# Half 1's input products of the long convolution beside its recurrence, and its gating beside its delta rule

## The chip, the cores and the metric

The kernel runs on one core of a Trainium2 chip. The metric is the device time of one execution in microseconds; of several runs of the kernel before, the median is 3470.67 us. The engines are TensorE (PE in the rows, PEld for its weight loads), VectorE (DVE), ScalarE (ACT), GpSimd (POOL) and SyncE (SP). Each engine works through its own list of instructions in order. Weights are loaded by SP, rows of the expert tables are gathered by GpSimd, and both kinds of transfer share the core's 16 DMA engines.

## The reference

512 tokens of 1024 features, in float32, go through three blocks: (1) feed-forward, a mixer, feed-forward; (2) a mixer and a product-key mixture of experts (PEER); (3) retention, a state-space scan and a feed-forward. The change concerns the two mixers of blocks 1 and 2. Cut to these:

```python
# block 1: proj = x @ w_in -> q, f, i, g, conv_val, conv_gate
f = lb + (1 - lb) * sigmoid(f_raw);  k = 1 - f;  log_f = log(f)
o = hgrn2_chunkwise(heads(q), heads(k), heads(i_val), heads(log_f))   # the recurrence
o_a = rms(o) * hgrn_norm_g * sigmoid(g_out)
u = conv_val * sigmoid(conv_gate)                                     # input of the convolution
c = depthwise_conv(u, conv_w, width=31) + conv_b                      # along the tokens
mix = concat([o_a, silu(layer_norm(c))]) @ w_out

# block 2: p = h @ w_in
uv = gelu(p[..., COL_GM:COL_Q]);  u, v = uv[..., :512], uv[..., 512:]
v = rms_norm(v, gm_norm_w)                                            # in chunks of 128, heads of 64
s = einsum('hts,bnshd->bnthd', tril(ws), v) + bs;  y_a = u * s        # the gating
qkv = silu(short_conv(p[..., COL_Q:COL_Z], conv_w))
o = gated_delta_rule(l2(q), l2(k), v, g, beta);  y_b = rms_norm(o) * silu(z)
x = x + gt1 * (concat([y_a, y_b]) @ w_out)
h2 = modulate(rms_norm(x));  ids, gates = peer_routing(h2)            # 8 heads, 16 experts each
ff = sum(gates * gelu(h2 . peer_u[ids]) * peer_v[ids])
```

## The kernel before

The tokens are handled in two halves of 256 (`self.hf` is 0 or 1), each of two tiles of 128, one half behind the other. First half 0 goes through blocks 1 and 2 up to the routing. Then `experts` runs the 512 gather steps of half 0's experts beside half 1's blocks 1 and 2, and after that half 1's experts beside half 0's block 3. This change lies in the first of these two stages for the most part: half 1's mixers run there while half 0's gather steps fill in.

A gather step (`gather_steps`, L1155) is a gather of 128 rows of 4 KB, 0.524 MB, issued by GpSimd (L1164) up to 8 steps ahead, and one use of it: a `u_step` multiplies and sums on DVE (L1171); a `v_step` adds a scaled row to the sum on DVE (L1194), or on PE as two 128x512 products with a diagonal (L1186 builds it on ScalarE, L1188 multiplies). After 16 u-steps ScalarE applies gelu (L1174).

Where the steps stand is decided when the program is built. `tick(d, load)` adds `d * z * rate` to a credit, less `load`, and lets steps in as long as the credit covers them; `z` and the share of v-steps on PE come from `ZONE` by phase (h the recurrence, d the delta rule, m the mixer of block 2). Every tile of weights ticks 3 with a load of 1.46, every PSUM tile ticks `self.beat`, which is 1.7 in the recurrence and in the delta rule and 0 elsewhere. A second means, `idle(d)`, takes pieces from a generator `self.side` when a PSUM tile is taken: `d` is `self.gap`, from `GAP`. Until now `side` served feed-forwards of the other half alone. In the end a scheduler puts the instructions of each engine into one list, and that list is what runs.

In half 1 products are whole float32 products (`self.exact`): one matmul instruction leaves two records in the trace. `g_fm` (L256) makes feature-major products, eight instructions for one weight tile, `g_tm` (L278) token-major ones, four a tile and half. A weight tile is 0.524 MB.

Around the change, the order in half 1 is as follows. `_hgrn` (L527): products f, then the input products of the convolution (L571 to L576: `pv` and `pg`, their sigmoid `csg`, the product into `uT`), then g, q, v; then the recurrence over the two tiles (from L591), in whose first steps k is transposed (L596), k and q are multiplied (L604), decays are summed by `Mseg` (L614) and products of decayed operands follow (L631); `head_norm` closes each tile. The convolution over `uT` follows. `_mixer2` (L790): products of q, k, v, gates of the delta rule, z; then `_gating` (L839): product v (L855), product u (L856), for each tile a normalisation (L859), the product with `ws` (L863), the bias (L865), the product with u (L867), then transposes (`put_mix`, L835); then `_delta` (L888). Its head loads the constants `PM`, `tri` and `later` (L170), sums g (L900), transposes q, k, v (L915, L935), and inverts a triangular matrix by doubling, level after level (L986, L992, L995), each a chain of three products with DVE and ScalarE between them.

In half 0 the same functions run with products in parts (L280 to L282), with no gather steps beside them.

Of the kernel before, what the change touches and what calls it, by code (L numbers as in the profile page):

```python
# [21 lines left out]
NT = 4          # token tiles  # L22
NH = 2          # token tiles of a half: the halves run one behind the other
# [11 lines left out]
# Costs of steps, in the unit of tick and idle: a transfer of 512 KB, a step of the routing, the end of a token tile  # L35
DMA, ROUTE, FINISH = 1.46, 0.8, 6.0
AHEAD = 8           # gathers under way ahead of their use
GB = 15             # their buffers
# the hidden blocks of the feed-forwards that run piece by piece in the gaps of the other half
ASIDE1 = (4, 4, 4, 4, 4, 2)  # L40
ASIDE3 = (4,) * 4
FIRST3 = 16          # hidden blocks of the third feed-forward of half 0 beside the last experts
ADA = 28             # tiles of the modulation beside the first feed-forward, the others beside the second
CONV_PE = (0, 2)     # blocks of the long convolution on TensorE, by half
# by phase: pace of the steps of the experts, share of their sums that TensorE takes
ZONE = dict(x=(1, 0.5), g=(1, 0.35), h=(1.15, 0.41), c=(0.43, 0.4), f=(1.43, 0), m=(1.73, 0.06), d=(1.09, 0.4),
            R=(1.09, 0.39), r=(1.33, 0.3), F3=(1.1, 0), s=(1, 0.65))
# pieces let in by gap of TensorE
GAP = dict(_0=4, l=3, h=0.74, c=0.22, m=5.53, d=0.9, r=0.5, s=1.6, _4=5.2, ln=8, l4=8)
NORM = 4.82          # pace of a normalisation  # L50
WEIGHTS = 3          # of a tile of weights in float32
# rates of the steps: modulation beside the two feed-forwards, experts during the routing
RATE_ADA, RATE_ROUTE = (0.85, 0.6), (0.92, 2.17)
# the course of the phases beside the experts, the transfers of their own, and the share of the experts' steps to fit in
# [3 lines left out]
class Ker:  # L58
    def __init__(self, ctx, tc, I):
# [3 lines left out]
        self.exact = False      # products in float32 itself, not in parts  # L63
# [14 lines left out]
        self.aux = nc.gpsimd        # for what VectorE need not do, unless GpSimd has transfers to start  # L78
        self.lull = self.gap = 0.0
        self.busy = False  # L80
        self.hook = None
        # states: of the first and of the second block, then both of the third block's retention
# [13 lines left out]
    def xt(self, es, side=None):  # L96
        """transposed activations, split in two, for one phase"""
        xp = es.enter_context(self.tc.tile_pool(name="xt", bufs=1, side=side))
        self.XH, self.XL = self.pair(xp, "X", KD)

    def pair(self, pool, name, n, **k):
        """an operand of products, n blocks: in two parts, or whole"""
# [22 lines left out]
    def course(self, i):  # L125
        """the rate that spreads the steps of the experts over a phase"""
        whole, loads, share = COURSE[i]
        self.rate, self.credit = (share * sum(f[0] for f in self.fill) + loads) / whole, 0.0

    def tick(self, d, load=0.0):  # L130
        """a phase goes on by d, with load for a transfer of its own: the steps of the other half's experts
        go in between so that the transfers are even"""
# [12 lines left out]
    def idle(self, d):  # L145
        """TensorE has little to do for d: pieces of the feed-forward set aside go in between"""
        if self.side is not None:
            self.lull += d
            while self.lull > 0.0 and self.side is not None:
                self.lull -= self.next_piece()  # L150

    def next_piece(self):
        d = next(self.side, None)
        if d is None:
            self.side = None
        return d or 0.0

# [18 lines left out]
    def rsqrt(self, out, in_, scale, eps):  # L176
        """out = (in_ * scale + eps) ** -0.5: Newton's iteration from the halved exponent"""
# [43 lines left out]
    def ahead(self):  # L221
        """of the weights of a feed-forward set aside, split the next tile and load on"""
# [9 lines left out]
    def whole(gen):  # L232
        """all pieces of a generator at once; its value"""
# [12 lines left out]
    def g_fm(self, srcs):  # L246
        """feature-major blocks: out[f, i, t] = sum_k w_i[k, f] X[t, k]; srcs [128, 8*128]"""
# [1706 lines left out]
```

## Time and profile before

| | us |
|---|---|
| median of the runs | 3470.67 |
| lowest and highest | 3467.29, 3487.89 |
| span of the profiled execution | 3464.7 |
| PE busy in it | 3023.7 (87%) |
| DVE busy | 2667.9 (77%) |
| GpSimd busy | 1439.0 (42%) |
| ScalarE busy | 1145.3 (33%) |

The span is that of one profiled execution, from its first to its last instruction. A row of the timeline gives start, duration, engine, line, operation, `out<-in`, shape and the count of equal instructions joined; in brackets the idle time before it and what ended that. A row of the windows gives the length, the busy time of each engine with its instructions, the granted PE clock (1.00 is 2.4 GHz), the share of the DMA engines in use and what they moved. The stage of half 1's first two blocks lies between about 1000 and 1930 us.

### The profile page before, as it was taken

The numbers are of one execution on the slowest core, as the hardware profiler recorded it, in microseconds if no ns is written. First come the engines' busy times: TensorE is split into PE (matmuls) and PEld (weight loads), VectorE is DVE, ScalarE is ACT, GpSimd is POOL, SyncE is SP. The second block draws the span as 40 slices with busy tenths as digits, with TensorE's granted clock in tenths as the row PEclk, the third lists the DMA queues.
The fourth block names the chain that finished last, engine by engine and source line by source line (L and its number), as shares of the span: only waits on it lengthen the run. The fifth ranks groups of instructions, "written<-read, shape, count | busy, mean of one in ns | idle before, by whom it ended". The sixth has DMA issues, their size and how long they took to land. (4 is left out here: it accounts for less than half of the span.)

```text
span 3464.7 us, 44842 instructions
## 1 busy us (share of the span) xinstructions
PE 3023.7 (87%) x15402; PEld 2350.9 (68%) x15402; DVE 2667.9 (77%) x6456; ACT 1145.3 (33%) x1687; POOL 1439.0 (42%) x1187
## 2 busy tenths in 40 slices
PE   9999999998979789987777867879797975999998
PEld 9987889888866357836354643536474745888897
DVE  7779686665588999878898999897877786566555
ACT  4454544553312242103222121112222213455554
POOL 0020000023245656655677567586767671211200
PEclk9999999999999899998899988899998987999999
DMA  8863477542389979998999899999999995644365
GB/s 312 279 194 118 131 267 233 168 161 86 105 303 357 355 263 384 409 402 325 381 326 375 335 339 391 347 368 357 333 365 359 396 409 193 182 133 139 119 188 162
DMA packets 276757, 957.10 MB, mean 276 GB/s; under 512 B 38304, under 2 KB 42144, under 8 KB 276528
## 3 DMA queue, kind: packets, MB, share of 16 engines
q0 software_dynamic: 147456, 536.94, 41.0%
q1 hardware_dynamic: 129072, 417.29, 35.6%
q8 instruction: 122, 2.00, 0.2%
q14 instruction: 107, 0.88, 0.1%
HBM read 947.81 MB, written 2.10 MB: 274 GB/s over the span
## 5 line engine op out<-in xcount | busy, mean ns | idle before, releaser
L1164 POOL DMA_INDIRECT gu<-in_peer_v,idx x512 | 633.6, 1238 | 317.1 <-issue 111.9
L1164 POOL DMA_INDIRECT gu<-in_peer_u,idx x512 | 609.3, 1190 | 349.6 <-issue 110.9
L1171 DVE SCALAR_TENSOR_TENSOR gu<-gu 128x1024 f32<-128x1024 f32 x512 | 620.7, 1218 | 59.4 <-DMA gu<-in_peer_u,idx 55.7
L203 DVE TENSOR_TENSOR wL<-wr,wH 128x1024 fp32r<-128x1024 f32 x332 | 409.1, 1234 | 249.2 <-ACT wH L202 231.9
L256 PE MATMUL ps<-XH,wr 128*128 128x256 f32 x2368 | 528.7, 383 | 0.2 <-issue 0.2
L256 PEld LDWEIGHTS ps<-XH,wr 128*128 128x128 f32 x2368 | 450.9, 192 | 73.2 <-issue 12.8
L202 ACT CAST wH<-wr 128x1024 fp32r<-128x1024 f32 x332 | 348.3, 1050 | 440.3 <-PE ps L281 217.4
L1194 DVE SCALAR_TENSOR_TENSOR gu<-gu,act 128x1024 f32<-128x1024 f32 x366 | 467.6, 1278 | 28.6 <-DMA gu<-in_peer_v,idx 23.4
L1188 PE MATMUL ps<-gu,dg 128*128 128x512 f32 x568 | 306.5, 664 | 101.8 <-DMA gu<-in_peer_v,idx 67.4
L1188 PEld LDWEIGHTS ps<-gu,dg 128*128 128x128 f32 x568 | 112.7, 212 | 206.9 <-issue 158.2
L278 PE MATMUL ps<-wr,XH 128*128 128x512 f32 x512 | 229.1, 601 | 0.0
L256 PE MATMUL ps<-XH,wH 128*128 128x256 f32 x1408 | 206.5, 289 | 16.3 <-ACT XH L116 10.0
L256 PE MATMUL ps<-XH,wL 128*128 128x256 f32 x1408 | 202.4, 287 | 1.5 <-DVE wL L203 1.2
L256 PE MATMUL ps<-XL,wH 128*128 128x256 f32 x1408 | 203.0, 288 | 0.2
L256 PEld LDWEIGHTS ps<-XH,wH 128*128 128x128 f32 x1408 | 186.6, 196 | 21.9 <-ACT XH L116 13.7
L256 PEld LDWEIGHTS ps<-XH,wL 128*128 128x128 f32 x1408 | 185.6, 196 | 2.9 <-DVE wL L203 2.7
L203 DVE TENSOR_TENSOR fL<-fr,fH 128x1024 fp32r<-128x1024 f32 x98 | 126.1, 1288 | 79.5 <-ACT fH L202 50.1
L256 PEld LDWEIGHTS ps<-XL,wH 128*128 128x128 f32 x1408 | 186.5, 197 | 0.6 <-DVE XL L118 0.6
L278 PEld LDWEIGHTS ps<-wr,XH 128*128 128x128 f32 x512 | 98.0, 193 | 122.7 <-issue 120.3
L202 ACT CAST fH<-fr 128x1024 fp32r<-128x1024 f32 x98 | 102.6, 1047 | 175.4 <-PE ps L256 58.7
L1186 ACT ACTIVATE dg<-ident,act 128x128 f32<-128x128 f32 x142 | 55.1, 400 | 312.3 <-PE ps L1188 246.5
L184 POOL TENSOR_TENSOR r<-rx,mhalf 128x1 f32<-128x1 f32 x18 | 11.9, 669 | 330.7 <-DVE rx L182 330.7
(618 smaller groups left out, 5462.4 us busy)
## 6 DMA issues: line engine op xcount, KB each, us to landing
wr<-in_wi_fm SPq DMA_DIRECT2D x112, 512.0 KB
wr<-in_wi_tm SPq DMA_DIRECT2D x96, 512.0 KB
wr<-in_wf SPq DMA_DIRECT2D x96, 512.0 KB
wr<-in_wo SPq DMA_DIRECT2D x64, 512.0 KB
wa<-in_wada SPq DMA_DIRECT2D x48, 512.0 KB
wr<-in_f2g SPq DMA_DIRECT2D x44, 512.0 KB
wr<-in_f2u SPq DMA_DIRECT2D x44, 512.0 KB
wr<-in_f2d SPq DMA_DIRECT2D x44, 512.0 KB
```

The costliest lines, as they stand in the source:

```text
L184: nc.gpsimd.tensor_tensor(out=out, in0=x, in1=self.mhalf[:p, :].to_broadcast(list(out.shape)), op=ALU.pow)
L202: self.nc.scalar.copy(H, raw)
L203: self.nc.vector.tensor_tensor(out=L, in0=raw, in1=H, op=ALU.subtract)
L256: nc.tensor.matmul(ps[:, i * TH:(i + 1) * TH], a[:, k * P:(k + 1) * P], b[:, k, :], start=n == 0, stop=n == KD * len(terms) - 1)
L278: nc.tensor.matmul(pss[t], lh[:, ts], wh, start=k == 0, stop=k == nk - 1)
L1164: nc.gpsimd.indirect_dma_start(out=g, out_offset=None, in_=I[src], in_offset=bass.IndirectOffsetOnAxis(ap=idx[:, s:s + 1], axis=0))
L1171: nc.vector.scalar_tensor_tensor(g, g, 1.0, h2, op0=ALU.mult, op1=ALU.mult, accum_out=st["act"][:, s:s + 1])
L1186: nc.scalar.activation(dg, self.ident, AF.Copy, scale=c)
L1188: nc.tensor.matmul(st["ps"][i], dg, g[:, i * 512:(i + 1) * 512], start="pe" not in st, stop=s == 127)
L1194: nc.vector.scalar_tensor_tensor(st["acc"], g, c, st["acc"], op0=ALU.mult, op1=ALU.add)
```

## The change

For half 1, the input products of the convolution become a generator `conv_in` that runs in the gaps of the recurrence, and `_gating` becomes a generator `g_gating` that runs in the gaps of the delta rule. `beside` makes a copy of the object for them, with its own pace set to zero and the `tick` of the original. What is left of them is drained before tile 0's `head_norm`. For both halves the gating's chain of normalisation, `ws` and bias now stands between the v and the u product, the u product multiplies straight into `vg`, and `ya` is gone. For half 0 the input products stay where they were. The transposes of the gated result come, for half 1, after the delta rule. To make room, `idx0` and `gate0` have one buffer instead of two. No number of the pace is changed.

```diff
+    def beside(self, gen):
+        o = copy.copy(self)
+        o.beat, o.gap, o.side, o.tick = 0.0, 0.0, None, self.tick
+        self.side, self.lull = gen(o), 0.0
@@ _hgrn
-        for b in range(0, 4, 2):
-            pv = self.gemm_fm([I["wi1_fm"][4 + b], I["wi1_fm"][5 + b]])
-            pg = self.gemm_fm([I["wi1_fm"][8 + b], I["wi1_fm"][9 + b]])
-            sg = hp.tile([P, 2, TH], F32, tag="qe", name="csg", bufs=1)
-            nc.scalar.activation(sg, pg, AF.Sigmoid)
-            nc.vector.tensor_tensor(out=uT[:, b:b + 2, 30:30 + TH], in0=sg, in1=pv, op=ALU.mult)
-        if self.hf == 0:
+        late = self.hf == 1
+        def conv_in(o):
+            for b in range(0, 4, 2):
+                pv = yield from o.g_fm([I["wi1_fm"][4 + b], I["wi1_fm"][5 + b]])
+                pg = yield from o.g_fm([I["wi1_fm"][8 + b], I["wi1_fm"][9 + b]])
+                sg = hp.tile([P, 2, TH], F32, tag="csg" if late else "qe", name="csg", bufs=1)
+                nc.scalar.activation(sg, pg, AF.Sigmoid)
+                nc.vector.tensor_tensor(out=uT[:, b:b + 2, 30:30 + TH], in0=sg, in1=pv, op=ALU.mult)
+        if not late:
+            self.whole(conv_in(self))
             self.aux.tensor_copy(self.ch1, uT[:, :, TH:TH + 30])
...
+        if late:
+            self.beside(conv_in)
...
+            if late:
+                self.drain_side()
             self.head_norm(hp, po, gt[:, t, :], 0, t)
@@ _mixer2
-        with tc.tile_pool(name="m2s", bufs=1) as sp:
-            self._gating(sp, lhsX)
-        with tc.tile_pool(name="m2d", bufs=1) as dp:
-            self._delta(dp, qkv, zz, g, bt)
+        if self.hf == 0:
+            with tc.tile_pool(name="m2s", bufs=1) as sp:
+                self.whole(self.g_gating(sp, sp))
+                self.idle(GAP["m"])
+            with tc.tile_pool(name="m2d", bufs=1) as dp:
+                self._delta(dp, qkv, zz, g, bt)
+        else:
+            with tc.tile_pool(name="m2s", bufs=1) as sp, tc.tile_pool(name="m2d", bufs=1) as dp:
+                self.beside(lambda o: o.g_gating(sp, dp))
+                self._delta(dp, qkv, zz, g, bt)
+                for t in range(NH):
+                    self.put_mix(0, t, self.box["gated"][:, t, :])
@@ _gating -> g_gating
         def evac_u(t, ps):
-            nc.scalar.activation(ya[:, t, :], ps, AF.Gelu_apprx_tanh)
+            u = junk.tile([P, 512], F32, tag="osq", name="gu_", bufs=1)
+            nc.scalar.activation(u, ps, AF.Gelu_apprx_tanh)
+            self.aux.tensor_tensor(out=vg[:, t, :], in0=u, in1=vg[:, t, :], op=ALU.mult)
...
-        self.gemm_tm([I["wi2_tm"][1, i] for i in range(4)], lhsX, evac_v)
-        self.gemm_tm([I["wi2_tm"][0, i] for i in range(4)], lhsX, evac_u)
-        sq = sp.tile([P, 512], F32, name="gsq")
+        yield from self.g_tm([I["wi2_tm"][1, i] for i in range(4)], self.lhsX, evac_v)
         for t in range(NH):
+            sq = junk.tile([P, 512], F32, tag="osq", name="gsq", bufs=1)
...
-            self.aux.tensor_tensor(out=ya[:, t, :], in0=ya[:, t, :], in1=vg[:, t, :], op=ALU.mult)
-        for t in range(NH):
-            self.put_mix(0, t, ya[:, t, :])
-        self.idle(GAP["m"])
+            yield 0.9
+        yield from self.g_tm([I["wi2_tm"][0, i] for i in range(4)], self.lhsX, evac_u)
+        if self.hf == 0:
+            for t in range(NH):
+                self.put_mix(0, t, vg[:, t, :])
+        self.box["gated"] = vg
@@ _delta
+            if self.hf == 1:
+                self.drain_side()
             self.head_norm(dp, po, zz[:, t, :], 4, t)
@@ peer_route
-        idx = [pp.tile([P, 128], U32, name=f"idx{t}") for t in range(NH)]
-        gate = [pp.tile([P, 8, 16], F32, name=f"gate{t}") for t in range(NH)]
+        idx = [pp.tile([P, 128], U32, name=f"idx{t}", bufs=1 + t) for t in range(NH)]
+        gate = [pp.tile([P, 8, 16], F32, name=f"gate{t}", bufs=1 + t) for t in range(NH)]
```

What this does to PE's list in half 1 is shown at two places; a row is one line of the program with its operation, operands and count of instructions. First the products of block 1's mixer, before: the 64 instructions `XH,wr` are the input products of the convolution, `wr,XH` are token-major products (g, v), the next `XH,wr` are q, and `ident,kk` opens the recurrence.

```order
L256 MATMUL ps<-XH,wr 128x256 x64
L278 MATMUL ps<-wr,XH 128x512 x8
L1188 MATMUL ps<-gu,dg 128x512 x2
L278 MATMUL ps<-wr,XH 128x512 x8
L256 MATMUL ps<-XH,wr 128x256 x24
L1188 MATMUL ps<-gu,dg 128x512 x2
L256 MATMUL ps<-XH,wr 128x256 x8
L278 MATMUL ps<-wr,XH 128x512 x12
L1188 MATMUL ps<-gu,dg 128x512 x2
L278 MATMUL ps<-wr,XH 128x512 x4
L596 MATMUL ps<-ident,kk 128x128 x4
L1188 MATMUL ps<-gu,dg 128x512
```

The changed kernel at the same place, whose line numbers are higher:

```order
L288 MATMUL ps<-wr,XH 128x512 x8
L1218 MATMUL ps<-gu,dg 128x512 x2
L288 MATMUL ps<-wr,XH 128x512 x8
L1218 MATMUL ps<-gu,dg 128x512 x2
L266 MATMUL ps<-XH,wr 128x256 x8
L612 MATMUL ps<-ident,kk 128x128 x4
L266 MATMUL ps<-XH,wr 128x256 x8
L620 MATMUL ps<-qT,kT 128x128 x4
L1218 MATMUL ps<-gu,dg 128x512 x2
L266 MATMUL ps<-XH,wr 128x256 x8
L630 MATMUL ps<-Mseg,lf 128x512
L266 MATMUL ps<-XH,wr 128x256 x8
```

The 64 instructions now come in groups of eight behind the v product, among the first steps of the recurrence's tile 0. Their weight tiles move on SP's list behind those of q and v.

Second, the delta rule's tile 0, from the first level of its doubling on (`xx,alv`, `pw,xt` and `xt,pw` are the products of a level). Before, the levels have only expert sums (`gu,dg`) between them:

```order
L979 MATMUL ps<-ident,xt 128x128 x4
L986 MATMUL ps<-xx,alv 128x128 x4
L992 MATMUL ps<-pw,xt 128x128 x4
L995 MATMUL ps<-xt,pw 128x128 x4
L1188 MATMUL ps<-gu,dg 128x512
L986 MATMUL ps<-xx,alv 128x128 x4
L1188 MATMUL ps<-gu,dg 128x512
L992 MATMUL ps<-pw,xt 128x128 x4
L995 MATMUL ps<-xt,pw 128x128 x4
```

The changed kernel there: `vg,ws` is the gating's product with ws, `wr,XH` is its u product.

```order
L889 MATMUL ps<-vg,ws 128x64 x8
L1020 MATMUL ps<-pw,xt 128x128 x4
L889 MATMUL ps<-vg,ws 128x64 x8
L1023 MATMUL ps<-xt,pw 128x128 x4
L288 MATMUL ps<-wr,XH 128x512 x2
L1014 MATMUL ps<-xx,alv 128x128 x4
L288 MATMUL ps<-wr,XH 128x512 x2
L1020 MATMUL ps<-pw,xt 128x128 x4
L1023 MATMUL ps<-xt,pw 128x128 x4
L288 MATMUL ps<-wr,XH 128x512 x2
```

Two of the u product's instructions now stand before each of the products `xx,alv` and `pw,xt` of a level, and the v product stands ahead of the delta rule's transposes. On SP's list the loads of `PM`, `tri` and `later` move from between the tiles of `wo` of this mixer to between those of `wo` of block 1's mixer.

## Rows read from the trace of the kernel before

**Rows 1.** of the page: the span, the engines, and the costliest groups of gather steps

```profile
span 3464.7 us, 44842 instructions
...
PE 3023.7 (87%) x15402; PEld 2350.9 (68%) x15402; DVE 2667.9 (77%) x6456; ACT 1145.3 (33%) x1687; POOL 1439.0 (42%) x1187
...
L1171 DVE SCALAR_TENSOR_TENSOR gu<-gu 128x1024 f32<-128x1024 f32 x512 | 620.7, 1218 | 59.4 <-DMA gu<-in_peer_u,idx 55.7
...
L1194 DVE SCALAR_TENSOR_TENSOR gu<-gu,act 128x1024 f32<-128x1024 f32 x366 | 467.6, 1278 | 28.6 <-DMA gu<-in_peer_v,idx 23.4
```

**Rows 2.** windows: us, busy PE, PEld, DVE, ACT, POOL, PEclk, DMA share, GB/s

```profile
1100.00:1120.00 20.00, 20.00 (x80) 14.93 (x79) 12.63 (x33) 2.87 (x5) 12.76 (x12) 1.00 1.03 409
...
1140.00:1160.00 20.00, 10.23 (x26) 5.46 (x27) 20.00 (x68) 6.29 (x12) 11.45 (x11) 0.66 0.92 333
```

**Rows 3.** windows from the gating to the end of delta tile 0

```profile
1660.00:1680.00 20.00, 11.32 (x21) 4.65 (x20) 15.23 (x22) 3.59 (x10) 12.62 (x10) 0.74 1.03 410
1680.00:1700.00 20.00, 16.71 (x66) 10.34 (x65) 14.90 (x43) 2.77 (x5) 13.98 (x15) 0.91 1.03 409
1700.00:1720.00 20.00, 9.08 (x25) 5.18 (x24) 14.52 (x45) 3.07 (x5) 11.72 (x11) 0.67 0.99 375
...
1760.00:1780.00 20.00, 14.10 (x72) 9.23 (x71) 19.28 (x47) 4.45 (x8) 16.04 (x14) 0.87 0.95 340
```

**Rows 4.** timeline of PE, then of ScalarE, products and recurrence

```profile
1060.70 27.79 PE L256 MATMUL ps<-XH,wr 128*128 128x256 f32 x128
...
1134.76 0.60 PE L596 MATMUL ps<-ident,kk 128*128 128x128 f32 x4
...
1148.20 2.08 PE L604 MATMUL ps<-qT,kT 128*128 128x128 f32 x8 [11.98 <-ACT kT L598]
...
1146.19 0.22 ACT L1174 ACTIVATE act<-act 128x16 f32<-128x16 f32 x1 [23.80 <-DVE gu L1171]
```

**Rows 5.** waits of DVE from 1095 to 1137 us: total, times, longest

```profile
DVE gu L1171 <- DMA gu<-in_peer_u,idx: 10.7, 8, 3.1
DVE gu L1194 <- DMA gu<-in_peer_v,idx: 1.3, 3, 0.6
```

**Rows 6.** timeline of PE, the gating of half 1

```profile
1647.40 17.33 PE L278 MATMUL ps<-wr,XH 128*128 128x512 f32 x40
...
1676.95 11.58 PE L278 MATMUL ps<-wr,XH 128*128 128x512 f32 x24
...
1690.08 3.68 PE L863 MATMUL ps<-vg,ws 128*128 128x64 f32 x32
1697.05 1.97 PE L835 MATMUL ps<-ident,ya 128*128 128x128 f32 x8 [3.29 <-DVE ya L867]
...
1707.54 0.57 PE L900 MATMUL ps<-g,tri 128*128 128x8 f32 x2 [5.10 <-DMA tri<-in_c_tri]
```

**Rows 7.** timeline of PE, delta rule, tile 0: its head and one level

```profile
1722.07 1.08 PE L935 MATMUL ps<-ident,tmq 128*128 128x128 f32 x4 [7.60 <-DVE rt L191]
...
1744.59 1.16 PE L986 MATMUL ps<-xx,alv 128*128 128x128 f32 x8 [0.93 <-DVE xx L997]
...
1748.36 1.02 PE L1188 MATMUL ps<-gu,dg 128*128 128x512 f32 x2
```

**Rows 8.** timeline of SP's queue (SPq): issues of constants

```profile
1699.43 0.43 SPq L170 DMA_DIRECT2D tri<-in_c_tri  x1
```

**Rows 9.** timeline of ScalarE, DVE and PE, the gating of half 0

```profile
747.93 1.09 ACT L854 ACTIVATE vg<-ps 128x512 f32<-128x512 f32 x2
...
753.06 1.42 DVE L860 SCALAR_TENSOR_TENSOR vg<-vg,r,gw 128x512 f32<-128x512 f32 x2 [0.59 <-POOL r L184]
...
758.68 3.68 PE L863 MATMUL ps<-vg,ws 128*128 128x64 f32 x32
```

**Rows 10.** groups of instructions of ScalarE by line: table loads

```profile
L616 ACT ACT_TABLE_LOAD x5 | 6.4, 1283 | 4.1 <-PE ps L614 4.0
```

**Rows 11.** timeline of GpSimd (POOL): half 1's first gather

```profile
1929.15 0.94 POOL L1164 DMA_INDIRECT gu<-in_peer_u,idx  x1 [19.77 <-PE ps L256]
```

More of the change, by code (lines that the diff above doesn't have):

```diff
@@ L79, in __init__ @@
         self.lull = self.gap = 0.0
+        self.inside = False
+        self.box = {}
         self.busy = False
@@ L148, in idle @@
             self.lull += d
-            while self.lull > 0.0 and self.side is not None:
+            while self.lull > 0.0 and self.side is not None and not self.inside:
                 self.lull -= self.next_piece()
     def next_piece(self):
+        self.inside = True
         d = next(self.side, None)
+        self.inside = False
         if d is None:
@@ L837, in put_mix, with g_gating @@
         self.fill_pair(pt4, self.cut(dst or (self.XH, self.XL), slice(None), slice(blk, blk + nb), ts))
-    def _gating(self, sp, lhsX):
+    def g_gating(self, sp, junk):
         nc, I = self.nc, self.I
-        ya = sp.tile([P, NH, 512], F32, name="ya")
         vg = sp.tile([P, NH, 512], F32, name="vg")
```

## The prediction

> **What bounds the kernel now.** I read the page first for the two engines with most work: TensorE (PE) is busy 87% of the span and VectorE (DVE) 77% [rows 1]. These are averages over stages, so next came the windows of 20 us around the two places that the change touches, both in the stage where half 1's blocks 1 and 2 run beside half 0's expert gathers. There the picture differs from the average. Around the recurrence, DVE is full (20.00 of 20) in a window where PE has 10.23 [rows 2]. Where the products run, it is PE that is full, while DVE falls to 12.63 and the transfers stand at 1.03 of what the 16 engines carry, 409 GB/s [rows 2]. In the gating, PE (9.08 to 16.71) and DVE (14.52 to 15.23) both have gaps and the transfers are at 1.03 again [rows 3]. So the stage alternates: products make PE and the transfers the bound, recurrences make DVE the bound. The work that fills DVE is the gather steps: 620.7 us for the 512 u-products and 467.6 us for the 366 v-sums, 1.218 and 1.278 us each [rows 1].
>
> The timeline and the waits say what ends the gaps. PE's longest gap in the recurrence, 11.98 us, ends with ScalarE's copy kT [rows 4], but that copy stands in ScalarE's queue behind the gelu of an expert head, which waited 23.80 us for DVE's u-products [rows 4]. DVE in turn waited 10.7 us for u-gathers and 1.3 us for v-gathers in the stretch before [rows 5]. In the gating, PE waits 5.1 us for the constant tri, 3.3 us for the product ya and, in the delta rule's head, 7.60 us for a reciprocal root [rows 6, 7].
>
> **The change, part by part.** *Input products of the convolution.* The 64 matmuls (128 records) take 27.79 us between the f and the g products [rows 4]. They go into the first loops of tile 0 of the recurrence, with their 8 weight tiles of 0.52 MB and two multiplies of 0.7 us. On PE alone that would give back 27.8 us. DVE gives back less. From the f product to the recurrence, counted in DVE's order, the gather operations fall from 45 to 40. That is 5 x 1.25 = 6.2 us, 1.4 us of multiplies, and the 12.0 us of waits for gathers: 19.6 us at most. By the transfers it is 8 tiles and 5 gathers, 13 x 0.524 MB at 409 GB/s = 16.7 us. I take 17. In the recurrence the gather operations rise from 47 to 57, and the multiplies come in: 10 x 1.25 + 1.4 = 13.9 us on a full DVE. From the convolution to z they fall from 181 to 178, 3.7 us less. Sum: -17 + 13.9 - 3.7 = about **-7 us** (from -10 to 0; at 0 the waits for gathers only move).
>
> *Gating.* Its products take 28.9 us (17.33 + 11.58), the products with ws 3.68 [rows 6]. From the gating's first product (1647.40 [rows 6]) to tile 0's first transposes of tmq (1722.07 [rows 7]) 74.7 us pass. In it DVE idles 4.77, 5.10 and 5.48 us in three windows [rows 3], 15.4 us; the rest, 59.3, is work. After the change 20 gather operations fewer stand there (36 to 16), 25 us, and 7 us of the gating's own, so 27 us of work are left. The loads of tri and later, issued at 1699 us behind wo's tiles [rows 8], now stand ahead of f2g's, in the middle of block 1, so that wait goes. By the transfers, 20 gathers and 8 tiles at 409 GB/s are 36 us; by DVE's work up to 74.7 - 27 = 48 us go. I take 38. Tile 0 of the delta rule receives 14 gather operations (34 to 48), 17.5 us, and the gating's 7 us, on a DVE at 19.28 of 20 [rows 3]: +24.5. PE receives 28.9 + 3.7 us there and in the head. The two transposes of the gated result now come behind the delta rule, 1.97 us [rows 6], +2; tile 1 loses one operation, -1. Sum: -38 + 24.5 + 1 = **-13 us** (from -24, all idle of DVE and the 5.1 us gone and the work equal, to +8, if PE's part must wait as the third rival has it).
>
> *The other half's steps.* The pace is not retuned, and tile 0 of the gating no longer lets steps in at its products. From the last uu of the delta rule to the routing the gather operations fall from 40 to 34. The whole difference up to the routing of half 1 is -5 - 6 = 11 operations on DVE, 4 of which went to PE as v-sums. The last stretch gets shorter by part of 6 x 1.25 = 7.5 us; I take **-5**. The 7 displaced steps fall into the stage of half 1's experts, at one transfer of 0.524 MB each, 1.28 us at 409 GB/s: **+9 us**.
>
> *Half 0.* Its gating is reordered: v product, then norm and ws products, then the u product. Before, the norm's chain (from gelu at 747.93 to the scale at 753.06, two of 0.7 us) ran under the u product, and PE ran 3.68 us of ws products at the end, with the bias and the product ya behind them [rows 9]. Now up to 6.5 us of the chain (747.93 to 754.4) can stop PE after v, while 3.68 us at the end go. Range -4 to +7, I take **+2**. The smaller idx0 and gate0 cost nothing: both tiles' readers in half 0 are done by then (tile 0's 256 steps precede tile 1's). Otherwise the new writer would wait for the last gather of tile 0.
>
> *Activation tables.* Sigmoid now stands between the recurrence's exponentials, and gelu inside the delta rule. A table load takes 1.283 us [rows 10]. Counted in ScalarE's order there are 120 of them before and after; in half 1's recurrence 5 come in, 6.4 us on an engine that is busy 2 to 6 of 20 us [rows 2], and as many go elsewhere, so the sum gets nothing. The Trainium skill, "ScalarE: Activation LUTs", section "Table sets: the hidden batching unit", speaks against this part: calls are to be batched by table set, and a change of set is put at about 2.7 us with its drain. By that page the recurrence would lose up to 13 us (an estimate, five changes on the path); the trace agrees on the load's 1.283 us, and shows no drain of its own.
>
> **Sum.** -7 - 13 - 5 + 9 + 2 = -14 us against the profiled execution, 3464.7 us. The median of the runs is 3470.67, 6 us higher (launch and spread lie in it), so the same step gives **3457 us**.
>
> **Rivals.** *1. The gaps take everything (faster).* All of DVE's idle time in the two places vanishes: 12.0 + 15.4 us, with 5 us for the four sums that go to PE, less half 0's 2: -30 us, and the displaced steps hide. For it speaks PE's idle time, 9.77 us in one window of the recurrence and 22.9 us in three of the gating [rows 2, 3]; against it that DVE is full where the work goes. The granted clock adds to it. It is 0.66 in the window at 1140, where PE stood still for 11.98 us, 0.74 at 1660 and 0.67 at 1700 us [rows 2, 3], towards 1.2 GHz, and the transposes x4 of tmq take 1.08 us there [rows 7] against 0.60 for the like of kk at the full clock [rows 4]. Products in these gaps would keep 2.4 GHz: 10.23 x 0.34 + 11.32 x 0.26 + 9.08 x 0.33 = 9 us of PE, a third to all of it on the path. Together -33 to -39: about **3435 us**. The Trainium skill, "TensorE: Matmul & The Clock Gate", section "Part 1: The HAM clock gate", has this as a rule: the array's clock is halved unless it is kept busy. The trace agrees with 0.66 to 0.74 behind the waits.
>
> *2. Nothing comes of it.* The transfers stand at 1.03 in both stretches and their bytes do not change; what leaves one place is paid in the other. Half 1's first nine u-gathers stand in GpSimd's queue 10 to 12 gathers earlier among half 0's last ones. That queue waited 19.77 us there for the routing [rows 11]; 12 gathers held behind it cost 12 x 1.28 = 15 us. -14 + 15 = +1: **3472 us**.
>
> *3. The delta rule's chain (slower).* In the doubling, each level of 3.8 us (from 1744.59 to 1748.36 [rows 7]) is a chain of three small products with an expert sum between them. Now two pairs of gating matmuls of 1.81 us (28.9 / 16 for one pair) stand ahead of them in PE's queue, in order, at four levels: 8 x 1.81 = 14.5 us, and the ws products twice, 3.7 us. If these 18 us stand on the chain, and a third of DVE's added 24.5 comes on top instead of under them: -14 + 18 + 8 = +12, **3483 us**. It decides from 14 us that are not covered. Against it: DVE's subtractions of each level stand behind gather steps of 1.25 us anyway, for which PE waited 0.93 us at this level [rows 7].
>
> **Chances.** Forecast 0.50, rival 1 0.25, rival 2 0.13, rival 3 0.12. One per cent is about what a measurement of this kernel can tell from no change: 3436 and 3505 us. Of rival 1 about 0.2 lies below 3436, and 0.02 of the forecast; above 3505 needs rival 3 with all of DVE's 24.5 on top instead of a third (+16) and half 0's +7, or GpSimd's 15 us beside it, 0.08. So faster 0.22, same 0.70, slower 0.08. The range of 8 in 10 goes from 3424, rival 1 with all of the clock's part (-39) and the last stretch's 7.5, to 3488, rival 3 with half 0's upper end. The likeliest case's own is 3443 to 3470.
>
> **What would show it.** Right: no x128 row of convolution products ahead of the recurrence, the 11.98 us wait gone, gating to tmq at about 37 us instead of 74.7, no wait for tri, tile 0 of the delta rule 24 us longer, DVE at 19 of 20 or more throughout. Wrong: DVE waits for PE in the doubling (rival 3), GpSimd's 19.77 us grows or is followed by more of half 0's gathers (rival 2), PE's wait of over 3 us behind half 0's v product, or DVE idling less with the stage over 25 us shorter (rival 1).

## The result, and the profile after

The changed kernel takes 3504.78 us (median of 5 runs, 3495.63 to 3508.97) against 3470.67 us. The ratio estimated from all runs is 1.0076, 95% interval [1.0051, 1.0102]; that of the medians alone is 1.0098. It is slower, by 0.5 to 1.0%, where -0.4% was forecast, and the median lies above the range's end of 3488. Measured a second time, on another occasion (both_again below), it is slower by less: 1.0041 [1.0028, 1.0053]. The profiled execution went from 3464.7 to 3495.6 us, 31 us more.

The page first: the busy times hardly move against [rows 1]; PE has 15 us more, DVE 6 us less.

```profile
span 3495.6 us, 44880 instructions
...
PE 3038.5 (87%) x15418; PEld 2363.3 (68%) x15418; DVE 2661.5 (76%) x6452; ACT 1146.0 (33%) x1691; POOL 1436.1 (41%) x1187
...
L1201 DVE SCALAR_TENSOR_TENSOR gu<-gu 128x1024 f32<-128x1024 f32 x512 | 622.4, 1220 | 55.2 <-DMA gu<-in_peer_u,idx 55.0
...
L1224 DVE SCALAR_TENSOR_TENSOR gu<-gu,act 128x1024 f32<-128x1024 f32 x362 | 463.3, 1280 | 24.1 <-DMA gu<-in_peer_v,idx 22.7
```

So the 31 us are waits, and have to be looked for by place. The starts of like instructions on PE, taken from the two traces, split the span as follows (the first stretch begins at PE's first product, 4.5 us into the span in both):

| stretch, by PE's list | before | after | difference |
|---|---|---|---|
| start to half 0's first transposes of tmq | 773.1 | 787.0 | +13.9 |
| to half 1's first norm | 264.9 | 266.5 | +1.6 |
| norm, f, (convolution), g, q, v products, to kk of tile 0 | 92.2 | 65.0 | -27.2 |
| recurrence, tile 0 | 67.6 | 92.2 | +24.6 |
| tile 1 to its last head | 40.5 | 41.1 | +0.6 |
| to the gates of block 2's mixer (wnr) | 385.1 | 387.7 | +2.6 |
| z, (gating), to tile 0's transposes of tmq | 94.1 | 52.1 | -42.0 |
| delta rule, tile 0 | 68.5 | 107.9 | +39.4 |
| tile 1 to the routing | 89.5 | 94.4 | +4.9 |
| routing to the end | 1584.6 | 1597.2 | +12.6 |

Both moves did what they are meant to: the stretches ahead got shorter by 27 and 42 us, and the tiles that took the work got longer by 25 and 39 us. So half 1's two mixers win nothing, where the forecast had them win some 25 us, and what lengthens the run is half 0, +14, and the stage after the routing, +13.

**Half 0.** The timeline of PE (start, duration, what; in brackets the wait and what ended it) answers to [rows 9]:

```profile
748.14 0.39 PE L292 MATMUL ps<-wL,XH 128*128 128x512 f32 x1
752.65 3.64 PE L889 MATMUL ps<-vg,ws 128*128 128x64 f32 x16 [4.12 <-DVE vg L886]
758.64 3.65 PE L889 MATMUL ps<-vg,ws 128*128 128x64 f32 x16 [2.34 <-DVE vg L886]
762.05 0.77 PE L290 MATMUL ps<-wH,XH 128*128 128x512 f32 x1
...
774.00 0.39 PE L292 MATMUL ps<-wL,XH 128*128 128x512 f32 x1
775.74 0.66 PE L861 MATMUL ps<-ident,vg 128*128 128x128 f32 x4 [1.35 <-POOL vg L878]
```

The first row is the last of the v product, 762.05 and 774.00 are the first and the last of the u product. The same places before:

```profile
746.85 0.39 PE L282 MATMUL ps<-wL,XH 128*128 128x512 f32 x1
747.08 0.39 PE L280 MATMUL ps<-wH,XH 128*128 128x512 f32 x1
...
758.45 0.40 PE L282 MATMUL ps<-wL,XH 128*128 128x512 f32 x1
758.68 3.68 PE L863 MATMUL ps<-vg,ws 128*128 128x64 f32 x32
763.05 0.65 PE L835 MATMUL ps<-ident,ya 128*128 128x128 f32 x4 [0.69 <-POOL ya L867]
```

Before, 32 records of the ws products took 3.68 us together. Now each half of them waits for the norm, 4.12 and 2.34 us, and takes 3.64 us by itself, as long as the whole did. The windows show the granted clock. Before:

```profile
744.00:764.00 20.00, 18.90 (x99) 15.34 (x97) 10.04 (x13) 11.05 (x16) 3.08 (x4) 1.00 0.61 196
```

and after:

```profile
744.00:764.00 20.00, 13.53 (x57) 11.88 (x57) 6.63 (x9) 5.58 (x9) 1.08 (x2) 0.67 0.34 105
```

The granted clock is 0.67 instead of 1.00 in the window in which PE stood still, and the DMA share falls with it. A half of the ws products takes twice what it took before (3.64 us against half of 3.68), which fits the lower of the clock's two levels, 1.2 instead of 2.4 GHz.

From the last start of v to the first of u 13.9 us now pass, where it was 0.2: the waits and the ws products, 4.12 + 3.64 + 2.34 + 3.65 = 13.75 us. The end gives back 2.9 us (from the last start of u to the transposes 1.74 us instead of 4.60). The other 3 us of the +13.9 stand in small pieces: 1.3 ahead of the end of v, 0.6 in u, 1.1 behind the transposes. The second wait, 2.34 us, is one of order: DVE takes up the second tile's root only behind the first tile's bias, which waits for PE's first ws product.

```profile
756.33 0.69 DVE L891 TENSOR_TENSOR vg<-ps,bs 128x512 f32<-128x512 f32 x1 [2.69 <-PE ps L889]
756.94 0.14 DVE L192 TENSOR_SCALAR rx<-r 128x1 f32<-128x1 f32 x1
```

**The recurrence.** The timeline of PE, which answers to [rows 4]:

```profile
1122.97 0.60 PE L612 MATMUL ps<-ident,kk 128*128 128x128 f32 x4
...
1131.76 2.08 PE L620 MATMUL ps<-qT,kT 128*128 128x128 f32 x8 [4.73 <-ACT kT L614]
...
1161.93 1.19 PE L647 MATMUL ps<-E 128*128 128x128 f32 x4 [5.95 <-DVE E L643]
...
1212.48 2.08 PE L1218 MATMUL ps<-gu,dg 128*128 128x512 f32 x2 [8.62 <-ACT dg L1216]
```

No x128 row is left ahead of kk. The 11.98 us wait has become 4.73 us, and two others grew: 5.95 us for DVE's E (1.57 at that place before) and 8.62 us ahead of an expert sum, for ScalarE's dg (5.27 before). The windows of the same stretch (us; busy PE, PEld, DVE, ACT, POOL; PEclk, DMA share, GB/s), which answer to [rows 2]:

```profile
1120.00:1140.00 20.00, 15.27 (x62) 11.86 (x61) 16.45 (x72) 1.39 (x4) 12.03 (x13) 0.83 1.03 409
1140.00:1160.00 20.00, 15.98 (x63) 11.47 (x61) 20.00 (x90) 8.21 (x11) 10.31 (x12) 1.00 1.03 408
```

PE's clock is back at 1.00 at 1140, as the first rival had it, but the stretches up to the end of tile 0 win only 2.6 us together (-27.2 + 24.6); the transfers stand at 1.03 in both windows.

**The delta rule.** PE, answering to [rows 6, 7]:

```profile
1675.06 0.57 PE L928 MATMUL ps<-g,tri 128*128 128x8 f32 x2 [11.88 <-DVE g L913]
...
1696.15 0.63 PE L963 MATMUL ps<-ident,tmq 128*128 128x128 f32 x4
```
```profile
1716.68 2.74 PE L1218 MATMUL ps<-gu,dg 128*128 128x512 f32 x6
1726.93 3.67 PE L889 MATMUL ps<-vg,ws 128*128 128x64 f32 x16 [7.51 <-DVE vg L886]
...
1732.21 2.75 PE L889 MATMUL ps<-vg,ws 128*128 128x64 f32 x16
...
1786.81 0.45 PE L861 MATMUL ps<-ident,osq 128*128 128x128 f32 x1 [5.80 <-issue]
...
1804.09 1.11 PE L963 MATMUL ps<-ident,tmq 128*128 128x128 f32 x4 [10.22 <-DVE tmq L955]
```

The wait for tri (5.10) is gone, and one for the gates g has its place, 11.88 us. In the first level of the doubling PE stands 7.51 us before the ws products, for DVE's scaled vg, and the level's next product stands behind them in the list. DVE's own rows show what is late:

```profile
1713.94 0.15 DVE L192 TENSOR_SCALAR rx<-r 128x1 f32<-128x1 f32 x1 [1.37 <-ACT gsq L727]
...
1719.35 1.23 DVE L1201 SCALAR_TENSOR_TENSOR gu<-gu 128x1024 f32<-128x1024 f32 x1
...
1720.49 0.23 DVE L200 TENSOR_TENSOR rt<-r 128x1 f32<-128x1 f32 x2
1720.64 1.28 DVE L1224 SCALAR_TENSOR_TENSOR gu<-gu,act 128x1024 f32<-128x1024 f32 x1
...
1725.93 0.23 DVE L202 SCALAR_TENSOR_TENSOR r<-rt,r 128x1 f32<-128x1 f32 x2
1726.13 1.41 DVE L886 SCALAR_TENSOR_TENSOR vg<-vg,r,gw 128x512 f32<-128x512 f32 x2
```

From 1713.94 to 1726.13 DVE computes the root of the norm, in small operations (a row of 0.15 to 0.23 us each), and in between it does eight gather steps of 1.2 to 1.3 us each that stand in its list, some 10 of the 12 us. The windows answer to [rows 3]:

```profile
1660.00:1680.00 20.00, 8.12 (x22) 4.19 (x21) 19.01 (x40) 4.17 (x6) 13.60 (x13) 0.66 1.03 405
1680.00:1700.00 20.00, 20.00 (x67) 9.91 (x65) 19.50 (x53) 3.87 (x8) 15.73 (x15) 1.00 1.03 408
1700.00:1720.00 20.00, 15.84 (x55) 9.53 (x52) 14.90 (x33) 9.27 (x16) 13.11 (x11) 0.83 0.99 390
1720.00:1740.00 20.00, 13.07 (x64) 11.23 (x65) 16.29 (x36) 1.20 (x3) 11.35 (x12) 0.74 0.82 301
...
1760.00:1780.00 20.00, 19.72 (x106) 13.33 (x105) 16.21 (x32) 5.17 (x11) 13.95 (x13) 1.00 0.99 370
```

DVE, full before the change in the delta rule (19.28), has 14.90, 16.29 and 16.21 of 20 there. The whole tile in one row, before and after:

```profile
1722.10:1790.50 68.40, 51.16 (x274) 36.24 (x274) 66.94 (x141) 18.58 (x33) 50.51 (x43) 0.90 0.91 315
```
```profile
1696.10:1804.10 108.00, 80.61 (x364) 54.74 (x363) 89.35 (x190) 21.96 (x43) 71.18 (x64) 0.87 0.92 347
```

DVE's work grew by 22.4 us, near the 24.5 of the forecast, and its idle time from 1.5 to 18.7 us.

### The profile page after: what moved, and what is told of

Same layout as the page of the kernel before. It is cut to its first block, busy times and chain, and to the rows that moved or that the text cites. A ratio compares the mean times of both kernels' runs of the same rounds, so it can differ in the third digit from the quotient of the medians.

```text
span 3495.6 us, 44880 instructions
## 1 busy us (share of the span) xinstructions
PE 3038.5 (87%) x15418; PEld 2363.3 (68%) x15418; DVE 2661.5 (76%) x6452; ACT 1146.0 (33%) x1691; POOL 1436.1 (41%) x1187
```

## The experiments

All are compared with the kernel before, run beside them on the same chip. There it took 3453 to 3454 us, and 3471 us (one run) beside the two trials without gather steps. Stretches are taken from the traces as in the table above, each from one profiled execution; where nothing else is said, the base is the trace of before_again, below. The single buffers of `idx0` and `gate0` stay in all these programs, so what they cost was not tried alone.

**Parts alone.** Half 0's order alone, both moves of half 1 undone:

```diff
-        late = self.hf == 1
+        late = False
...
-        if self.hf == 0:                      # in _mixer2: gating ahead of the delta rule in both halves
+        if True:
...
+        early_u = self.hf == 1                # in half 1 the u product right behind v, as before
```

> Only half 0's gating in the changed order (v product, norm and ws products, u product); both moves of half 1 are undone. Theory A (the norm's chain stops TensorE behind v, and the splits of u's weights on ScalarE stop with it): +14 us, a span near 3479 us, and the whole of it between 745 and 780 us. Theory B (this place is covered later by slack, and the loss comes from half 1's two moves alone): within 3 us of the kernel before, 3465 us.

Measured: 3458.97 against 3453.63 us, ratio 1.0013 [1.0001, 1.0024]; at its place +14.3 us (788.4 against 774.1 us). The place is as theory A said, and it is clear of the scatter: the eleven traces with the old order have 771.4 to 779.9 us there, the three with the new one 784.5 to 788.4. The end time shows less, 4.5 us (0.3 to 8). The profiled execution, 3466.77 us, was the slowest of the ten, and even in it the stage from the routing to the end is 7 us shorter than before (1576.5 against 1583.6 us), though nothing of half 1 is moved and 462 gather steps are done at its start in both. How much of the 14 us later slack gives back is therefore not settled.

The other way round, only this order undone in the changed kernel:

```diff
+        early_u = self.hf == 0
+        ya = sp.tile([P, NH, 512], F32, name="ya") if early_u else None
...
+        if early_u:
+            yield from self.g_tm([I["wi2_tm"][0, i] for i in range(4)], self.lhsX, evac_u)
```

> The changed kernel with half 0's gating put back in its old order. Theory A: 14 us less than the changed kernel, a span near 3482 us, still 17 us above the kernel before. Theory B: no change, 3495 us.

Measured: 3452.77 us, 1.0004 [0.9990, 1.0018]; half 0's stretch is back at 775.7 us. Without half 0's order the change is worth nothing, and nothing is lost either: the 17 us that theory A left over were not there.

The convolution's products alone (gating in both halves as before it, ahead of the delta rule):

```diff
-        if self.hf == 0:                      # in _mixer2
+        if True:
...
+        early_u = True
```

> Only the input products of the convolution beside half 1's recurrence; both gatings as before. Theory A (what the products' stretch gives back, 26 us, comes back in tile 0 as gather steps, routing steps and waits for gathers): 0 to +3 us, 3465 to 3468 us, the recurrence's end within 2 us of where it was. The prediction's term of -7 us: 3458 us. Theory B (moves of half 1 cost 31 us between them): +10 us or more.

Measured: 3445.18 us, 0.9975 [0.9965, 0.9984], 8.5 us faster. At its place nothing is won: norm to last head 195.0 us against 193.0. Three more gather steps are done when half 1's routing begins (465 against 462), and the stage behind it is 9 us shorter in the profile (1574.3 us). So theory A was right on the place and wrong on the time. The forecast's -7 was right on the time by luck: h0_order, which moves no products, wins 7 us in that stage too.

Half 1's gating alone:

```diff
-        late = self.hf == 1
+        late = False
...
+        early_u = self.hf == 0
```

> Only half 1's gating beside its delta rule; half 0's gating in its old order, the input products as before. Theory A: delta tile 0 grows by about 39 us against 40 us won ahead of it, and some 10 gather steps fall behind the routing, +12 us: 3478 to 3482 us. The prediction's terms (-13 - 5 + 9): 3456 us. Theory B: +20 us or more, 3485 us.

Measured: 3437.39 us, 0.9947 [0.9927, 0.9966], 16 us faster by the medians, on the prediction's side. z to tmq went from 90.2 to 47.8 us, tile 0 from 70.8 to 97.8, tile 1 to the routing from 89.1 to 96.3: 8 us less at the place of the move (11 in the repeat below). Another 8 us are won from the routing to the end (1575.3 us), as in h0_order.

The two parts alone give -8.5 and -16 us, and both together, in h0_undone, nothing. How much of that is scatter was the next question.

**The kernel before and the changed one once more.**

> The kernel before, unaltered, as a run of its own: the ratio is the error of the comparison (1.000 within 0.002 by either theory), and its trace gives the stages of the kernel before on the chip on which the others of this call run.

Measured: 1.0003 [0.9992, 1.0014]. Its trace is the base for the stretches.

> The changed kernel, unaltered, once more. Theory A (its loss is half 0's reorder, 14 us at its place and 4 to 5 in the end time, with the two moves of half 1 worth nothing together): ratio 1.001 to 1.003, +4 to +10 us. Theory B (the loss of 26 us belongs to the program and comes from all three parts together): ratio 1.006 or more.

Measured: 3467.38 against 3453.02 us, 1.0041 [1.0028, 1.0053]. It lies between the two theories (the median is 14 us higher); half 0's stretch has +10.4, and the three stretches of gating and delta rule sum to -3.2 instead of +2.3 us. Routing to end is 1583.4 against 1583.6 us: the 12.6 us of the first measurement are not there.

**The ws products later.** The norm's chain stays where it is, but the loop over the two tiles is split behind it, and the two ws products, with the u product behind them, are let in some nine PSUM tiles later:

```diff
             nc.vector.scalar_tensor_tensor(vg[:, t, :], vg[:, t, :], r, gw, op0=ALU.mult, op1=ALU.mult)
+        if self.hf == 1:
+            yield 8.0
+        for t in range(NH):
             ps = self.psum()
```

> Half 1's gating alone beside the delta rule, as in gating_alone, but its two products with ws (and with them its u product) stand some nine PSUM tiles later in TensorE's order. Theory C (ws stands at the head of TensorE's queue while VectorE works through the root of the norm between gather steps, and the doubling's next product waits behind it): the wait of 2 to 7.5 us ahead of ws goes, delta tile 0 gets 3 to 7 us shorter than in gating_alone, the ratio goes from 0.9947 to about 0.993. Rival D (VectorE's gather steps set the pace there anyway): tile 0 within 2 us, ratio as in gating_alone.

Measured: 3432.38 us, 0.9943 [0.9921, 0.9964]. Tile 0 took 93.0 us against 97.8 (94.1 in a repeat, below), so 1 to 5 us; the time does not tell it from gating_alone.

> Both moves of half 1, half 0's gating in the old order, and the ws products of half 1 some nine PSUM tiles later. Theory C: 3 to 7 us less than h0_undone, ratio about 0.999. Rival D: ratio 1.000 as in h0_undone.

Measured: 3435.49 us, 0.9949 [0.9932, 0.9966], against 1.0004 without the shift (0.9985 in a repeat, below): 12 to 17 us by the medians, more than theory C asked for, and with intervals that do not meet. In the changed kernel on the same chip PE waited here:

```profile
1711.29 3.67 PE L889 MATMUL ps<-vg,ws 128*128 128x64 f32 x16 [4.05 <-DVE vg L886]
```

and with the shift:

```profile
1695.14 1.16 PE L1032 MATMUL ps<-pw,xt 128*128 128x128 f32 x8 [0.73 <-ACT pw L1028]
...
1701.17 1.90 PE L898 MATMUL ps<-vg,ws 128*128 128x64 f32 x16
...
1704.71 1.90 PE L898 MATMUL ps<-vg,ws 128*128 128x64 f32 x16
```

The wait of 4.05 us is gone, and the ws products take 1.90 us instead of 3.67: the clock had not fallen. DVE's root takes 12 us here too (1687.25 to 1699.34), but PE has the doubling's products ahead of it meanwhile. The whole tile in one row, first the changed kernel, then with the shift:

```profile
1685.90:1784.80 98.90, 76.55 (x362) 51.37 (x362) 88.97 (x190) 21.79 (x43) 67.88 (x63) 0.90 0.98 374
```
```profile
1674.90:1760.70 85.80, 72.35 (x357) 47.60 (x356) 82.73 (x183) 21.48 (x42) 68.21 (x53) 0.95 0.99 372
```

98.9 us became 85.8, DVE's idle time 9.9 us became 3.1, and PE's clock rose from 0.90 to 0.95. The rest of the 13 us, 6 us of DVE's work, is six of the tile's 60 gather steps that fell to tile 1, which absorbed them: from there to the routing it took 89.6 us (94.4 before the shift), with the same 456 steps done. So theory C holds where both moves are made: the ws products at the head of PE's list, waiting for the norm's chain, cost the delta rule's tile its idle time, and with it the win. With gating alone it is worth little, and why it is worth less there is not shown.

**Without the gather steps.** To see what bounds the recurrence, no steps were let in during half 1's mixer, in the kernel before and in conv_alone:

```diff
+        self.busy = self.hf == 1              # tick returns at once
         self.gemm_tm([I["wi1_tm"][0, i] for i in range(4)], lhsX, evac_f)
...
         self.beat = 0.0                       # behind the last head
+        self.busy = False
```

> The kernel before, but no gather step of half 0's experts is let in during half 1's recurrence mixer, from its f product to its last head (they all run later; nothing is left out). It is the base for hold_conv: the f product to the recurrence's end took 193 us with the steps in. Theory E (steps set the pace): without them it falls by 20 us or more. Rival F (TensorE's own work and the recurrence's chain set it): less than 10 us.

> conv_alone with the same hold. Theory E (with the steps in, the stretch from the f product to the recurrence's end is bound by the transfers and VectorE, whose work the move leaves as it is, so that it gave +2 us): with the steps out, the move of the 28 us of products into the recurrence's gaps pays, 15 us or more of the stretch against hold_before. Rival F (the products delay the recurrence's own chain on TensorE whatever runs beside it): within 5 us of hold_before.

Measured: 3635.24 and 3648.68 us, one run each. From the norm to the last head hold_before takes 177.6 us against 193.0 with the steps, 15 us less, which lies between its two theories. hold_conv takes 174.6 us there, 3 us less than hold_before, which is what rival F asked for; the 15 us of theory E did not come. The trial doesn't separate the causes all the same, since DVE was full: 59 gather operations still ran between 1040 and 1200 us, beside the routing and the convolution's taps. And up to the sums of the convolution's norm hold_conv is the longer one, 218.4 against 208.6 us from the f product (with the steps 224.9 and 222.3). A window of hold_before, from the f product to kk:

```profile
1048.00:1130.70 82.70, 82.70 (x291) 54.73 (x290) 82.70 (x228) 17.67 (x28) 29.02 (x25) 1.00 0.80 290
```

DVE is busy 82.70 of 82.70 us, at a DMA share of 0.80. The trial shows one thing beside: the 62 operations of the convolution on DVE (29 us) ran from 1081 to 1105 us in hold_before, and from 1135 to 1180 us in hold_conv. They need the input products, and go where these go, from under the g and q products into the recurrence. With the steps in, they stood in the recurrence either way (first at 1141 and 1143 us).

**The two moves together once more.**

> h0_undone once more (both moves of half 1, half 0's gating in the old order). Theory G (the two moves together lose what gating_alone wins, and the loss is a property of the program): ratio 0.998 to 1.002 again, and the stretch from half 1's routing to the end 5 to 8 us longer than in gating_again. Theory H (the difference of 15 us between them was the scatter of a chip): ratios of the two within 0.002.

> gating_alone once more (only half 1's gating beside the delta rule, half 0's in the old order). Theory G: ratio 0.993 to 0.996. Theory H: within 0.002 of undone_again.

Measured: 0.9985 [0.9973, 0.9997] and 0.9968 [0.9956, 0.9980], 6 us apart instead of 15. By the ratios that is theory H: they lie within 0.002, and the intervals overlap, so most of the 15 us was scatter. The stretch from the routing to the end is as theory G says: it repeats within 2 us for each program (1582.5 and 1583.9 with both moves, 1575.3 and 1577.5 with gating alone). It is not a loss of the two moves, though: the kernel before takes 1583.6 us there, as long as they. Shorter are the programs with one part alone, 1574.3 to 1578.5 us, and h0_order, which moves nothing in half 1, is one of them. So which length the stage behind the routing has follows neither from the moved work nor from the steps done at its start (462 in h0_order as before; 456 and 455 in the two programs here). Which difference in the lists makes it is open.

## Why the prediction was wrong

The terms of the forecast beside what the two traces of the changed kernel show, each against a trace of the kernel before (us; the second is both_again against before_again):

| term | forecast | first measurement | second |
|---|---|---|---|
| half 0 | +2 | +13.9 | +10.4 |
| to half 1's first norm | 0 | +1.6 | +0.4 |
| products and recurrence | -3.1 | -2.0 | +3.4 |
| from there to block 2's gates | -3.7 | +2.6 | +0.7 |
| gating, delta rule, to the routing | -18 | +2.3 | -3.2 |
| displaced steps, routing to the end | +9 | +12.6 | -0.2 |
| sum | -14 | +31.0 | +11.5 |

The largest miss is the gating's, 15 to 20 us; half 0's, 8 to 12 us, is what turns a change worth nothing (h0_undone) into a loss.

**Half 0.** The term was +2 with a range to +7. The working named the chain (6.5 us of waits, which is what it cost: 4.12 + 2.34) and then took off 3.68 us for ws products that would go at the end. The end did give back 2.9 us. But the same products now stand between v and u, on PE's path, which the term put at nothing, and at half the clock behind the waits they take 7.3 us there. The prediction's own sign for this, a wait of over 3 us behind v, came with 4.12 us. The clock's cost was worked out for half 1 as a gain, from the same rows, and not for half 0 as a loss.

**The convolution, -7.** The 17 us expected ahead of the recurrence were 27.2 (25.9 in the second measurement), and the 13.9 expected in tile 0 were 24.6 (25.8). The two errors are one. The prediction had 5 gather operations leave the one stretch and 10 come into the other; between the marks of the table twelve steps leave (68 to 56 done at kk) and twelve come back. With the 8 weight tiles these are 20 transfers of 0.524 MB, by its own 409 GB/s 25.6 us, on either side. In the second measurement DVE is busy 146.1 of 157.4 us from the norm to the end of tile 0 before the change, and 146.7 of 157.3 after, and 114 gather steps are done at that point either way:

```profile
1040.80:1131.30 90.50, 90.50 (x322) 59.66 (x321) 79.57 (x268) 24.18 (x37) 49.75 (x43) 0.99 0.97 369
1131.30:1198.20 66.90, 47.38 (x164) 25.82 (x163) 66.55 (x192) 15.28 (x30) 47.10 (x42) 0.83 0.96 350
```
```profile
1051.60:1116.20 64.60, 64.60 (x206) 37.61 (x205) 59.10 (x175) 21.18 (x33) 36.06 (x31) 0.99 0.96 349
1116.20:1208.90 92.70, 72.75 (x281) 48.19 (x280) 87.58 (x288) 22.47 (x37) 59.32 (x55) 0.91 0.97 375
```

Neither DVE's work nor the transfers up to there changed (DMA share 0.96 to 0.97 in each row), and the time did not either. PE's idle time in tile 0 stayed too, 19.5 and 20.0 us: the products did not fill it. The step that failed is that 12 us of waits for gathers would vanish with the products and not come back. That is the second rival's mechanism, what leaves one place is paid in the other, and the end 0 of the term's own range. That the transfers set the time, rather than DVE, fits the 25.6 us but is not shown: in hold_before they stand at 0.80, and the move gains only 3 us to the last head. In conv_alone the forecast's time came out, 8.5 us, but behind the routing, where h0_order wins 7 us without the move.

**The gating, -13.** The 38 us ahead were right in size (42.0, and 36.7 in the second measurement), though the wait for tri that was to go was followed by one of 11.88 us for the gates g. Tile 0 was put at +24.5 and came to +39.4 and +28.1. The sum of DVE's work was right, that it stays full was not, and this is the step that failed: DVE idled 18.7 us in the tile, 9.9 in the second measurement. The third rival had the mechanism, PE's list in order before the doubling's products, but with the wrong instructions. The pairs of the u product, which need nothing, stood there without a wait; the ws products, which need DVE's root, held up the level by 4 to 7.5 us and cost the clock too. both_ws_later shows it, 12 to 17 us with these products let in later. The last stretch was put at -4 with the transposes and came to +4.9: the gather operations that left it won nothing; why is not shown. (The term's lower bound, -24, does not follow from what it names: 15.4 and 5.1 us make 20.5.)

**Displaced steps, +9.** Six steps fell behind the routing, where 7 were expected. In the first measurement the stage grew by 12.6 us, in the second by nothing, and with gating alone it is 6 to 8 us shorter than before with seven displaced steps, so the runs do not bear out the price of 1.28 us a step. GpSimd's wait for the routing (19.77 before [rows 11]) is 21.18 us after, and a wait for PE's expert sum stands ahead of it that the forecast has not (2.57 us in before_again):

```profile
1902.34 0.94 POOL L1194 DMA_INDIRECT gu<-in_peer_v,idx  x1 [11.05 <-PE ps L1218]
...
1945.65 0.94 POOL L1194 DMA_INDIRECT gu<-in_peer_u,idx  x1 [21.18 <-DVE mrep L1268]
```

In the second measurement the stage takes 1583.4 against 1583.6 us with both waits in it (11.06 and 21.19 us), so the second rival's 15 us did not come.

**Tables.** ScalarE's trace has 120 table loads before and after, as the prediction counted. What it costs to have five of them inside the recurrence was not tried alone.

**What stays open.** Why the same program lost 0.76% in one measurement and 0.41% in the other, if it did: the intervals just overlap, and tile 0 of the delta rule took 107.9 and 98.9 us. In the first PE and DVE show idle time there that the trace puts down to no wait, 5.80 us ahead of osq among it. Nor is it known what makes the stage behind the routing shorter in some programs, and longer by 12.6 us in the first measurement.

A version better than both kernels came out of it: half 1's gating alone beside the delta rule, with the ws products later, at 0.9943 [0.9921, 0.9964] of the time before, or both moves with that shift at 0.9949 [0.9932, 0.9966], half 0's gating in its old order in either.

## What to carry to other kernels

Work that is put into an engine's gaps must be ready when its turn comes: an instruction that waits for another engine, put between the links of a chain, holds up the chain, and in an ordered list it pays its wait with everything behind it, here with the clock as well. Before counting a gap as free, add up what the two sides of the move need in transfers and on the engine that is full; here that sum did not change over the whole stretch, and neither did its time (157.4 and 157.3 us). And when a chain is moved off the end of a stage, ask where its instructions stand now, not only what it no longer covers.

## What the hardware showed

Sixteen records of the ws products took 3.64 us behind a standstill of 4.12 us, at a granted clock of 0.67 over that window, and 1.90 us in both_ws_later, where PE had been busy. So the fall of the clock behind a wait of 4 us cost another 1.7 us. The kernel before took 3470.67 us in the first measurement and 3453 to 3454 us on three chips later (3471 us in one run on a fourth), 0.5% apart, so a kernel is best compared with one that ran beside it on the same chip.
